# Branch B of a streaming layer: a segment's cast, subtraction and transfer given out two segments later

## The chip, the cores and the metric

The kernel runs on one core of a Trainium2 chip. The metric is device microseconds of one launch, as the median of several runs; lower is better. A profiled execution, taken by the hardware profiler, shows which engine did what and when: TensorE (PE), VectorE (DVE), ScalarE (ACT), GpSimd (POOL), and SyncE (SP), which issues the DMAs here.

## The reference, cut to what matters

One layer with two token mixers side by side. Branch A is a differential attention with softmax, branch B a stick-breaking attention; a gated merge and an output projection follow. There are 2048 prompt rows and 128 sample rows (8 running streams of 16). The change touches branch B's prompt rows alone:

```python
def stick_breaking_attention(q, k, v, qpos, kpos):
    z = jnp.einsum('bqhd,bkhd->bhqk', q, k,
                   preferred_element_type=jnp.float32) * (HEAD_DIM_B ** -0.5)
    mask = kpos[None, :] < qpos[:, None]
    log_1m = jnp.where(mask, jax.nn.log_sigmoid(-z), 0.0)
    log_a = jax.nn.log_sigmoid(z) + lax.cumsum(log_1m, axis=3, reverse=True) - log_1m
    a = jnp.where(mask, jnp.exp(log_a), 0.0)
    o = jnp.einsum('bhqk,bkhd->bqhd', a, v, preferred_element_type=jnp.float32)
    return o.astype(v.dtype)
```

In other words: the weight of key k is sigmoid(z_k) times the product of sigmoid(-z) over all later keys that the mask admits. The kernel computes that running product with a scan from the last key to the first.

## The kernel before

**Units and tiles.** The work is eight units, u = 0 to 7, one for each pair of heads (two of branch B, c = 0 and 1) and branch: the even ones are branch A, the odd ones branch B. A unit goes through 17 tiles of 128 rows, the sample tile (t = NT = 16) first and then t = 0 to 15. For each tile it projects, stores gates, and computes scores; tile t of the prompt has t + 1 key blocks of 128. While one unit's scores run, the projections of the next are interleaved, so that PE has other work between score matmuls; unit 7 is the last and has less of it. The second part of the kernel (branch and output projections, sample rows) follows unit 7 from about 1751 us on.

**One segment.** A head's keys are cut into segments of up to SEG = 8 blocks (1024 keys). A tile from 8 to 15 has two per head: segment 0 with 1024 keys, and segment 1 with the last 128 to 1024. A head's scores come in chunks of 512 keys from the last to the first; each goes through this chain:

- PE: score matmuls (L701, L702) into one of three PSUM banks `ps_s`
- ACT: two sigmoids (L599 and L600, shown as L135, since `act` records them): sigmoid(z) into the buffer `sc_p`, sigmoid(-z) back into the bank
- DVE: the scan (L675) of the bank into the buffer `sc_n`; a copy of one column (L674) carries it from segment 1 to segment 0

Behind a head's last chunk `stick_weights` is called for segment 1 and then segment 0: POOL multiplies `sc_p` by the shifted `sc_n` (L681). Then comes `turn`, which makes the weights ready for PE: ACT casts them to 16 bits (L609), DVE subtracts the cast from the exact weights (L612) for a low half, and SP issues a transposing DMA of both halves into `wt` (L619). From there PE multiplies with the values (L762, L763), 27 units of `later_on` behind (PV_LAG).

**What sets the order.** `later_on(lag, fn)` puts a piece of work on a list that `give` works off as work is given out; `spent` counts the cost of what has been given. `turn` is given out 1.5 plus up to 1 behind `stick_weights`; in unit 7 and for sample tiles at once. A scheduler then moves instructions within the dependencies; instructions marked `kept` stay in program order on their engine. The cast is kept for u < 7, the subtraction is not kept. The buffers `sc_p` and `sc_n` have 6 each, `wt` 5.

L725 is a gate's multiplication, L743 scales an output tile, L324 scales the values, L246 to L249 belong to later scales: all short DVE instructions that stand between scans and subtractions.

Of the kernel before, what the change touches and what calls it, by code (L numbers as in the profile page):

```python
# [22 lines left out]
ALU = mybir.AluOpType  # L23
# [10 lines left out]
NT = SEQ // P  # L34
# [5 lines left out]
SEG = 8  # L40
PV_LAG = 27.0
TURN_LAG = 1.5
B_LAG = 1.5
EXP_LAG = 1.0
SUM_LAG = 2.0
PIECE, CHUNK, PV_A, PV_B = 0.44, 0.22, 0.17, 0.085
# [79 lines left out]
def layer_kernel(ctx: ExitStack, tc: tile.TileContext, a: dict):  # L126
    nc = tc.nc
    V, S, G, T = nc.vector, nc.scalar, nc.gpsimd, nc.tensor
# [12 lines left out]
    def kept(x):  # L141
        tc.keep_in_program_order(x)
        return x
# [172 lines left out]
    def split(hi, lo, src, s, on=None):  # L316

        if on is S:
            S.activation(out=hi, in_=src, func=AF.Identity, scale=s)
        elif on is G:  # L320
            G.tensor_scalar(out=hi, in0=src, scalar1=s, scalar2=0.0, op0=ALU.mult, op1=ALU.add)
        else:
            V.tensor_scalar(out=hi, in0=src, scalar1=s, scalar2=None, op0=ALU.mult)
        V.scalar_tensor_tensor(out=lo, in0=src, scalar=s, in1=hi, op0=ALU.mult, op1=ALU.subtract)  # L324
# [277 lines left out]
    def turn(job, seg, scale=None):  # L602

        nb = seg["hi"] - seg["lo"]
        nk = nb * P
        w16 = seg["n"].bitcast(F16)
        hi, lo, src = w16[:, 0:nk], w16[:, nk : 2 * nk], seg["p"][:, 0:nk]
        if scale is None:
            x = S.copy(out=hi, in_=src)  # L609
            if job["t"] < NT and job["U"]["u"] < 7:  # L610
                kept(x)
            V.tensor_tensor(out=lo, in0=src, in1=hi, op=ALU.subtract)  # L612
        else:
            split(hi, lo, src, scale, S)
        if job["t"] == NT:
            seg["wt"] = job["pool"].tile([P, 10, P], F16, tag="dwt", name="dwt", bufs=2)
        else:
            seg["wt"] = wtp.tile([P, 2 * SEG, P], F16, tag="wt", name="wt", bufs=WT_BUFS)
        nc.sync.dma_start_transpose(out=seg["wt"][:, 0 : 2 * nb, :], in_=w16[:, 0 : 2 * nk])  # L619
        if job["t"] < NT:  # L620
            cost = (PV_A, PV_B)[job["U"]["kind"]]
            for fn in pv(job, seg):
                later_on(PV_LAG, fn, cost)

    def softmax_pair(job):
# [8 lines left out]
        def powers(i, c):  # L634
            seg = segs[i]
            w = seg[("p", "n")[c]][:, 0 : (seg["hi"] - seg["lo"]) * P]
            act(out=w, in_=w, func=AF.Exp, bias=nm[:, c : c + 1], accum_out=l[:, c, i : i + 1])
# [9 lines left out]
        def joined(seg):  # L647
            nk = (seg["hi"] - seg["lo"]) * P
            p, n = seg["p"][:, 0:nk], seg["n"][:, 0:nk]
            x = V.scalar_tensor_tensor(out=p, in0=n, scalar=r[:, 2:3], in1=p, op0=ALU.mult, op1=ALU.add)  # L650
            if job["t"] < NT:
                kept(x)

        stages = [(EXP_LAG, lambda i=i, c=c: powers(i, c)) for i in range(len(segs)) for c in range(2)]
        stages.append((EXP_LAG + SUM_LAG + 2.0 * n_all, sums))
        for i, seg in enumerate(segs):
            at = EXP_LAG + SUM_LAG + 2.0 * n_all + i
            stages += [(at, lambda seg=seg: joined(seg)), (at + TURN_LAG, lambda seg=seg: turn(job, seg, r[:, 0:1]))]
# [19 lines left out]
    def stick_weights(job, seg, later):  # L678
        m = (seg["hi"] - seg["lo"]) * P - (later is None)
        p, n = seg["p"], seg["n"]  # L680
        G.tensor_tensor(out=p[:, 0:m], in0=p[:, 0:m], in1=n[:, 1 : m + 1], op=ALU.mult)  # L681
        if job["t"] == NT or job["U"]["u"] == 7:
            turn(job, seg)
        else:
            later_on(B_LAG + m / 1024, lambda: turn(job, seg))

    def scores(U, t, jobs):

# [5 lines left out]
        def chunk(c, ch):  # L694
            job = own[c if kind == 1 else 0]
            seg = job["segs"][ch * 4 // SEG]
            n = 512 if ch < t // 4 else (t % 4 + 1) * P
            p = bank("s")
            qst, kk = U["q", t], U["k"][ch]
            diag = ch == t // 4  # L700
            T.matmul(p[:, 0:n], qst[:, c, :], kk[:, c, 0:n], start=True, stop=False)  # L701
            T.matmul(p[:, 0:n], qst[:, 2 + c, :], kk[:, c, 0:n], start=False, stop=not diag)  # L702
            if diag:
                m = mask_a if kind == 0 else mask_b
                T.matmul(p[:, n - m.shape[1] : n], idb, m, start=False, stop=True)  # L705
            evacuate(job, seg, c, p, ch * 512 - seg["lo"] * P, n, sc[:, 3:4], sc[:, 4:5], ch)
            if kind == 0:
                if diag and c == 1:
                    softmax_pair(job)
                return  # L710
            i = job["segs"].index(seg)
            later = job["segs"][i + 1] if i + 1 < len(job["segs"]) else None
            stick(seg, later, ch * 512 - seg["lo"] * P, n, p)
            if ch * 4 == seg["lo"]:
                if later is not None:
                    stick_weights(job, later, None)
                if i == 0:
                    stick_weights(job, seg, later)
# [48 lines left out]
    def later_on(lag, fn, cost=0.0):  # L767

        spent[1] += 1
        bisect.insort(due, (spent[0] + lag, spent[1], cost, fn))  # L770

    def pv(job, seg):

        U, t, c, i = job["U"], job["t"], job["c"], job["segs"].index(seg)
        last_seg = len(job["segs"]) - 1 if U["kind"] == 0 else 0
        first_seg = 0 if U["kind"] == 0 else len(job["segs"]) - 1
        nb = seg["hi"] - seg["lo"]

        def block(j):
            first, last = i == first_seg and j == 0, i == last_seg and j == nb - 1  # L780
            if first and (U["kind"] == 0 or c == 0):
                U["po", t] = bank("o")
            pv_block(job, seg, U["po", t], j, U["v"][seg["lo"] + j], first, last)
            if last and (U["kind"] == 0 or c == 1):
                store(U, t, natural(U, t, U.pop(("po", t))))

        return [lambda j=j: block(j) for j in range(nb)]
# [14 lines left out]
    def sample(U, dec, qpad, cs, vs, parity):  # L802
# [34 lines left out]
        def scores_all():  # L837

            box["jobs"] = [new_job(U, t, c, 5, dec) for c in range(heads)]
            qsam, kn = box["s"][:, 0:4, :], box["s"][:, 4:6, :]  # L840
            mask = mask_as if kind == 0 else mask_bs
            pn = bank("t")
            for c in range(2):
                p = pn[:, c * P : (c + 1) * P]
                T.matmul(p, qsam[:, c, :], kn[:, c, 0:P], start=True, stop=False)
                T.matmul(p, qsam[:, 2 + c, :], kn[:, c, 0:P], start=False, stop=False)
                T.matmul(p, idb, mask, start=False, stop=True)
            for c in range(2):
                pc = bank("s")
                for b in range(2):  # L850
                    for f in range(2):
                        for i in range(4):
                            T.matmul(pc[i * 32 : i * 32 + 32, :], qpad[:, f * 2 + c, 2 * i + b, :], box["k", i][:, b * 4 : b * 4 + 4, c, :],  # L853
                                     start=(b == 0 and f == 0), stop=(b == 1 and f == 1))
                job = box["jobs"][c % heads]
                seg = job["segs"][0]
                evacuate(job, seg, c, pn[:, c * P : (c + 1) * P], 512, P, sc[:, 3:4], sc[:, 4:5], 1)
                evacuate(job, seg, c, pc, 0, 512, box["f"][:, 0:1], box["f"][:, 1:2], 0)
                if kind == 1:
                    stick(seg, None, 512, P, pn[:, c * P : (c + 1) * P])  # L860
                    stick(seg, None, 0, 512, pc)
                    stick_weights(job, seg, None)
            if kind == 0:
                softmax_pair(box["jobs"][0])
# [550 lines left out]
    for n in range(len(steps) + 2):  # L1415
        made, qk, side = [], [], []
        if n < len(steps):
            u, t = steps[n]
# [16 lines left out]
        if at[0] == len(line) and not spare and not cached:  # L1435
            m = n - len(steps)
# [201 lines left out]
```

## Time and profile before

| | |
|---|---|
| median of 3 runs | 2212.37 us (2209.06 to 2217.97) |
| the profiled execution | 2207.3 us |
| its span, first to last instruction | 2205.4 us |
| mean granted TensorE clock | 0.984 |
| start of the first and the last subtraction of tiles 8 to 15 | 381.5 and 524.8 us (unit 1), 790.1 and 934.0 (3), 1197.3 and 1345.1 (5), 1606.8 and 1742.4 (7) |

The table of waits names first who waited, then, behind the arrow, what ended the wait. A row of the windows gives a stretch, its length and each engine's busy time in it. A row of the timeline gives start, duration, engine, line, operation, and in brackets how long its engine sat idle before it and what released it. Names have their buffer numbers left out.

### The profile page before, as it was taken

To read this page: it belongs to the slowest core of one execution; us is meant where nothing else is said; L and a number is where in the kernel's file an instruction comes from. 1 tells how busy PE (TensorE), PEld (TensorE's weight loads), DVE (VectorE), ACT (ScalarE), POOL (GpSimd) and SP (SyncE) were. 2 spreads that over 40 slices of the span, in tenths; PEclk is the share of its full clock that TensorE was granted. 3 is DMA by queue.
4 is the path that set the end of the run, shared out by engine and by line. 5 is a ranking of instruction groups with operands and counts; after the bars stand their busy time and mean duration, and the time that the engine had idled before them with its cause. 6 is when DMAs were issued, how large, how long until landed. Compare 5 with 4: busy or idle time off the path is not lost. (4 is left out here: it accounts for less than half of the span.)

```text
span 2205.4 us, 40973 instructions
## 1 busy us (share of the span) xinstructions
PE 2044.0 (93%) x14504; PEld 1091.4 (49%) x14504; DVE 1734.5 (79%) x3651; ACT 1598.9 (72%) x3080; POOL 726.7 (33%) x618
## 2 busy tenths in 40 slices
PE   3999999999999999999999998999997799999997
PEld 1545555555555455555555545455554344444443
DVE  5668868889877887987878887787789778778874
ACT  3977677788877777978687788875687656666641
POOL 0433024466301444742034464402344412112220
PEclk9999999999999999999999999999999899999999
DMA  9778668899797999978888899885777899998862
GB/s 331 259 249 191 132 151 231 184 222 206 199 243 174 221 191 208 214 197 216 204 223 202 186 229 217 216 198 123 171 154 157 204 254 222 245 246 236 227 161 67
DMA packets 820814, 449.96 MB, mean 204 GB/s; under 512 B 551962, under 2 KB 759114, under 8 KB 820096
## 3 DMA queue, kind: packets, MB, share of 16 engines
q1 hardware_dynamic: 819660, 446.96, 82.1%
q8 instruction: 113, 1.85, 0.3%
q14 instruction: 93, 0.76, 0.1%
q10 hardware_dynamic: 948, 0.39, 0.1%
HBM read 229.87 MB, written 86.02 MB: 143 GB/s over the span
## 5 line engine op out<-in xcount | busy, mean ns | idle before, releaser
L681 POOL TENSOR_TENSOR sc_p<-sc_p,sc_n 128x127 f32<-128x127 f32 (+7 forms) x192 | 319.3, 1665 | 557.8 <-DVE sc_n L675 528.4
L466 PEld LDWEIGHTS <-hs 128*128 128x128 f16 x3120 | 292.8, 99 | 316.8 <-issue 9.1
L466 PE MATMUL ps_mm<-wa,hs 128*128 128x512 f16 x1590 | 390.5, 381 | 6.8 <-DMA hs<-hT_d 3.7
L466 PE MATMUL ps_mm<-wb,hs 128*128 128x512 f16 x1530 | 380.9, 380 | 0.0
L675 DVE TENSOR_TENSOR_SCAN sc_n<-ps_s,sc_n,zero_t 128x512 f32<-128x512 f32 x192 | 245.3, 1278 | 40.3 <-ACT ps_s L135 34.5
L612 DVE TENSOR_TENSOR sc_n<-sc_p,sc_n 128x128 f16<-128x128 f32 (+7 forms) x192 | 224.7, 1173 | 39.3 <-ACT sc_n L609 38.5
L701 PE MATMUL ps_s<-k,qst 128*128 128x512 f16 (+3 forms) x640 | 223.1, 349 | 32.2 <-DVE sc_n L675 27.8
L540 PEld LDWEIGHTS <-hs 128*128 128x128 f16 x1632 | 155.3, 98 | 184.2 <-DVE qst L569 4.8
L540 PE MATMUL ps_t<-wa,hs 128*128 128x512 f16 x1020 | 243.4, 381 | 1.1 <-DVE qst L569 0.7
L135 ACT ACTIVATE sc_p<-ps_s,usc 128x512 f32<-128x512 f32 (+3 forms) x320 | 205.7, 643 | 45.6 <-PE ps_s L702 34.2
L702 PE MATMUL ps_s<-k,qst 128*128 128x512 f16 (+3 forms) x640 | 223.1, 350 | 0.0
L609 ACT CAST sc_n<-sc_p 128x128 f16<-128x128 f32 (+7 forms) x192 | 155.9, 814 | 87.4 <-POOL sc_p L681 86.8
L135 ACT ACTIVATE ps_s<-ps_s,usc 128x512 f32<-128x512 f32 (+3 forms) x320 | 198.0, 619 | 0.0
L540 PE MATMUL ps_t<-wb,hs 128*128 128x512 f16 x612 | 150.5, 382 | 6.2 <-DMA hs<-hT_d 2.6
L1533 PE MATMUL ps_o<-wo,wb 128*128 128x512 f16 x672 | 151.1, 380 | 0.7 <-ACT wb L1307 0.7
L762 PE MATMUL ps_o<-v,wt 128*128 128x128 f16 x1088 | 133.1, 223 | 19.6 <-DMA wt<-sc_n 18.9
L1538 POOL TENSOR_TENSOR x<-m,x 128x512 f32<-128x512 f32 x32 | 45.9, 1434 | 249.5 <-DVE m L1536 174.1
L595 DVE TENSOR_SCALAR_CACHE_REDUCE sc_p<-ps_s,usc 128x512 f32<-128x512 f32 (+3 forms) x160 | 106.2, 664 | 24.1 <-PE ps_s L702 18.2
L763 PE MATMUL ps_o<-v,wt 128*128 128x64 f16 x1088 | 124.2, 195 | 0.0
L595 DVE TENSOR_SCALAR_CACHE_REDUCE sc_n<-ps_s,usc 128x512 f32<-128x512 f32 (+3 forms) x160 | 106.3, 664 | 22.7 <-PE ps_s L705 11.7
L762 PEld LDWEIGHTS <-wt 128*128 128x128 f16 x1088 | 100.1, 100 | 48.3 <-DMA wt<-sc_n 24.1
L1499 PEld LDWEIGHTS <-wa 128*128 128x128 f16 x816 | 77.9, 99 | 92.6 <-issue 7.8
(373 smaller groups left out, 4451.0 us busy)
## 6 DMA issues: line engine op xcount, KB each, us to landing
hs<-hT_d SPq DMA_DIRECT2D x132, 512.0 KB, 4.7
g_d<-gt SPq DMA_DIRECT2D x68, 256.0 KB, 4.0
out_dram<-pr SPq DMA_DIRECT2D x204, 64.0 KB, 3.9
o_d<-o SPq DMA_DIRECT2D x136, 64.0 KB, 3.2
wa<-g_d SPq DMA_DIRECT2D x17, 512.0 KB, 6.8
wb<-g_d SPq DMA_DIRECT2D x17, 512.0 KB, 5.3
hs<-o_d SPq DMA_DIRECT2D x17, 512.0 KB, 3.8
wide<-in_w_ada_dram SPq DMA_DIRECT2D x8, 1024.0 KB, 11.8
```

What stands on the lines that cost most here:

```text
L135: i = S.activation(**kw)
L466: T.matmul(box["p"], box["h"][:, hi, k, :], U["w"][k][:, wi, :], start=(n == 0), stop=(n == 3 * KT - 1))
L540: x = T.matmul(box["g"][:, 0:gw], box["h"][:, hi, k, :], U["wg"][k // per][:, k % per, wi, :], start=(j == 0), stop=(j == 3 * KT - 1))
L595: V.tensor_scalar(out=dst[:, lo : lo + n], in0=p[:, 0:n], scalar1=sc_pos, scalar2=None, op0=ALU.mult, op1=ALU.max, accum_out=job["mx"][:, ...
L609: x = S.copy(out=hi, in_=src)
L612: V.tensor_tensor(out=lo, in0=src, in1=hi, op=ALU.subtract)
L675: V.tensor_tensor_scan(out=dst[:, lo : lo + n][:, ::-1], data0=src[:, 0:n][:, ::-1], data1=zero_t[:, 0:1].to_broadcast([P, n]), initial=fi ...
L681: G.tensor_tensor(out=p[:, 0:m], in0=p[:, 0:m], in1=n[:, 1 : m + 1], op=ALU.mult)
L701: T.matmul(p[:, 0:n], qst[:, c, :], kk[:, c, 0:n], start=True, stop=False)
L702: T.matmul(p[:, 0:n], qst[:, 2 + c, :], kk[:, c, 0:n], start=False, stop=not diag)
L762: T.matmul(po[:, c * P : (c + 1) * P], wt[:, wj, :], vt[:, c, :, :], start=first, stop=False)
L1533: T.matmul(po, st["y"][:, yi * 8 + k, :], wo[j * 4 + k // 2][:, wi, k % 2, :], start=(n == 0), stop=(n == 3 * KT - 1))
```

## The change

For tiles 8 to 15 of branch B, `turn` no longer goes to the list `due` (or, in unit 7, out at once). A list `held` takes the segments; whenever it has more than TURN_BEHIND = 2, the oldest is turned. A head's two segments are thus turned when the next head's are multiplied. Behind the unit's last segment the remaining two are given out as before. The cast is now kept in program order in unit 7 too, and the subtraction is kept, both for t >= 8. Tiles below 8 and the sample tile go as before.

```diff
+TURN_BEHIND = 2
...
             x = S.copy(out=hi, in_=src)
-            if job["t"] < NT and job["U"]["u"] < 7:
+            y = V.tensor_tensor(out=lo, in0=src, in1=hi, op=ALU.subtract)
+            if job["t"] < NT and (job["U"]["u"] < 7 or job["t"] >= SEG):
                 kept(x)
-            V.tensor_tensor(out=lo, in0=src, in1=hi, op=ALU.subtract)
+            if SEG <= job["t"] < NT:
+                kept(y)
...
         G.tensor_tensor(out=p[:, 0:m], in0=p[:, 0:m], in1=n[:, 1 : m + 1], op=ALU.mult)
-        if job["t"] == NT or job["U"]["u"] == 7:
+        if job["t"] == NT:
+            turn(job, seg)
+        elif job["t"] < SEG:
+            give_turn(job, seg)
+        else:
+            held.append((job, seg))
+            if len(held) > TURN_BEHIND:
+                turn(*held.pop(0))
+            if job["t"] == NT - 1 and job["c"] == 1 and seg["lo"] == 0:
+                while held:
+                    give_turn(*held.pop(0))
+
+    held = []
+
+    def give_turn(job, seg):
+
+        if job["U"]["u"] == 7:
             turn(job, seg)
         else:
-            later_on(B_LAG + m / 1024, lambda: turn(job, seg))
+            later_on(B_LAG + (seg["hi"] - seg["lo"]) / SEG, lambda: turn(job, seg))
```

What moves, first on DVE, in unit 3 around the first head of tile 13. Line numbers of the kernel before: L675 is the scan (a `128x256` one opens a head of this tile), L612 the subtraction, L568 and L569 copies of the next tile's keys and queries.

```order
L675 SCALAR_TENSOR_TENSOR sc_n<-ps_s,sc_n,zero_t 128x512
L674 COPY sc_n<-sc_n 128x1
L612 TENSOR_TENSOR sc_n<-sc_p,sc_n 128x1024
L568 COPY k<-ps_t 128x2x128
L569 COPY qst<-ps_t 128x512
L675 SCALAR_TENSOR_TENSOR sc_n<-ps_s,sc_n,zero_t 128x512 x2
L743 SCALAR_TENSOR_TENSOR o<-ps_o,usc_8072,ob 128x128
L612 TENSOR_TENSOR sc_n<-sc_p,sc_n 128x768
L675 SCALAR_TENSOR_TENSOR sc_n<-ps_s,zero_t 128x256
L324 SCALAR_TENSOR_TENSOR v<-ps_mm,usc_11034,v 128x2x64
L612 TENSOR_TENSOR sc_n<-sc_p,sc_n 128x1024
```

The same place in the changed kernel (the scan is L678 here, the subtraction L611, the copies L569 and L570):

```order
L678 SCALAR_TENSOR_TENSOR sc_n<-ps_s,sc_n,zero_t 128x512
L569 COPY k<-ps_t 128x2x128
L677 COPY sc_n<-sc_n 128x1
L570 COPY qst<-ps_t 128x512
L678 SCALAR_TENSOR_TENSOR sc_n<-ps_s,sc_n,zero_t 128x512 x2
L611 TENSOR_TENSOR sc_n<-sc_p,sc_n 128x640
L611 TENSOR_TENSOR sc_n<-sc_p,sc_n 128x1024
L678 SCALAR_TENSOR_TENSOR sc_n<-ps_s,zero_t 128x256
```

Before, single subtractions stand between scans, those of 768 and 1024 columns for the head that has just been scanned. Now a pair stands behind the head's last scan, and it is tile 12's second head's (640 and 1024 columns); the pair of the head just scanned follows one head later.

At the end of unit 7, on DVE, from the last head's second chunk on (L244 to L249 are short instructions for later scales):

```order
L675 SCALAR_TENSOR_TENSOR sc_n<-ps_s,sc_n,zero_t 128x512
L743 SCALAR_TENSOR_TENSOR o<-ps_o,usc_18672,ob 128x128
L674 COPY sc_n<-sc_n 128x1
L675 SCALAR_TENSOR_TENSOR sc_n<-ps_s,sc_n,zero_t 128x512
L612 TENSOR_TENSOR sc_n<-sc_p,sc_n 128x1024
L675 SCALAR_TENSOR_TENSOR sc_n<-ps_s,sc_n,zero_t 128x512
L612 TENSOR_TENSOR sc_n<-sc_p,sc_n 128x1024
L244 TENSOR_SCALAR sc_q<-ps_t 128x8
L246 TENSOR_SCALAR sc_f<-sc_q 128x8
L248 TENSOR_SCALAR sc_e<-sc_f 128x8
L249 TENSOR_SCALAR sc_e<-sc_f 128x8
L612 TENSOR_TENSOR sc_n<-sc_p,sc_n 128x1024
```

And in the changed kernel:

```order
L678 SCALAR_TENSOR_TENSOR sc_n<-ps_s,sc_n,zero_t 128x512
L677 COPY sc_n<-sc_n 128x1
L678 SCALAR_TENSOR_TENSOR sc_n<-ps_s,sc_n,zero_t 128x512
L245 TENSOR_SCALAR sc_q<-ps_t 128x8
L678 SCALAR_TENSOR_TENSOR sc_n<-ps_s,sc_n,zero_t 128x512
L247 TENSOR_SCALAR sc_f<-sc_q 128x8
L249 TENSOR_SCALAR sc_e<-sc_f 128x8
L611 TENSOR_TENSOR sc_n<-sc_p,sc_n 128x1024
L250 TENSOR_SCALAR sc_e<-sc_f 128x8
L611 TENSOR_TENSOR sc_n<-sc_p,sc_n 128x1024 x2
L762 SCALAR_TENSOR_TENSOR o<-ps_o,usc_18672,ob 128x128
L611 TENSOR_TENSOR sc_n<-sc_p,sc_n 128x1024
```

Four subtractions stand behind the last scan where two stood. SP's transfers for them move with them. Before, among its last issues (L1323, L548, L1317: loads and stores of other stages, L752: an output tile's store):

```order
L619 DMA_TRANSPOSE wt<-sc_n 128x16x128
L1323 DMA wb_1406<-g_d_97 128x2x512
L619 DMA_TRANSPOSE wt<-sc_n 128x16x128 x2
L548 DMA g_d_108<-gt_1396 128x512
L1317 DMA hs_181<-z_d_80 128x512
L752 DMA o_d_76<-o 128x128
L619 DMA_TRANSPOSE wt<-sc_n 128x16x128
```

And in the changed kernel, where the transfer is L622:

```order
L622 DMA_TRANSPOSE wt<-sc_n 128x16x128
L1342 DMA wb_1406<-g_d_97 128x2x512
L549 DMA g_d_108<-gt_1396 128x512
L622 DMA_TRANSPOSE wt<-sc_n 128x16x128 x4
L1336 DMA hs_181<-z_d_80 128x512
```

The last tile's four transfers now stand in a row, and one load and one store that stood ahead of the last of them come behind.

## The prediction

> **What bounds the kernel now.** I read the page's engine shares first, then the windows of the late tiles, where segments are longest, then what PE waited for in each of them.
>
> ```profile
> span 2205.4 us, 40973 instructions
> PE 2044.0 (93%) x14504; PEld 1091.4 (49%) x14504; DVE 1734.5 (79%) x3651; ACT 1598.9 (72%) x3080; POOL 726.7 (33%) x618
> ```
>
> PE is busy 2044.0 of 2205.4 us: 161 us are all that a change of order can win anywhere. The change touches only branch B's tiles 8 to 15, so the windows show how much of that lies there: tiles 8 to 11 of unit 1, tiles 12 to 15 of units 1 and 5, then unit 7 from tile 11 to its end, in two pieces (each row: window, its length, busy times, clock, DMA share, GB/s).
>
> ```profile
> core 0: us, PE busy (x) PEld busy (x) DVE busy (x) ACT busy (x) POOL busy (x), PEclk, DMA share, GB/s
> 373.80:439.80 66.00, 66.00 (x468) 35.05 (x467) 53.99 (x79) 50.08 (x96) 27.34 (x21) 1.00 0.83 193
> 439.80:518.90 79.10, 75.54 (x574) 41.30 (x572) 70.90 (x83) 71.22 (x132) 51.11 (x35) 1.00 0.96 214
> ...
> 1254.80:1335.50 80.70, 75.49 (x567) 40.74 (x564) 69.57 (x83) 71.31 (x132) 50.25 (x35) 1.00 1.00 210
> 1644.40:1716.10 71.70, 54.29 (x450) 30.53 (x447) 69.19 (x78) 55.54 (x101) 38.16 (x21) 0.95 0.73 155
> 1716.10:1751.00 34.90, 23.11 (x175) 13.05 (x176) 24.89 (x39) 20.88 (x31) 16.23 (x8) 0.80 0.84 179
> ```
>
> Tiles 8 to 11 have PE busy 66.00 of 66.00 us: nothing to win. In tiles 12 to 15, PE is idle for 3.6 us (unit 1) and 5.2 us (unit 5). In unit 7, with less other work for PE in between, DVE is busy 69.19 of 71.70 us (96%) and PE only 54.29. So units 1, 3 and 5 are bound by PE with small holes, unit 7 by DVE. What fills the holes, as waits of PE (us in all, times, longest), in the same order with unit 3 after unit 1, each over the tiles of its window and on to the unit's last PV matmuls:
>
> ```profile
> engine line waited for: us in total, times, longest us
> PE ps_s L701 <- DVE sc_n L675: 3.6, 5, 1.5
> PE ps_o L762 <- DMA wt<-sc_n: 2.3, 2, 1.3
> ...
> PE ps_s L701 <- DVE sc_n L675: 3.5, 4, 1.5
> PE ps_o L762 <- DMA wt<-sc_n: 0.3, 1, 0.3
> ...
> PE ps_o L762 <- DMA wt<-sc_n: 4.6, 5, 3.2
> PE ps_s L701 <- DVE sc_n L675: 3.9, 3, 1.5
> ...
> PE ps_s L701 <- DVE sc_n L675: 14.8, 17, 2.4
> PE ps_o L762 <- DMA wt<-sc_n: 11.7, 7, 2.9
> ```
>
> Two waits matter: a score matmul (L701) for a PSUM bank that a late scan (L675) still holds, and a PV matmul (L762) for a transfer (L619).
>
> **The change, part by part.** No instruction is added or removed; casts, subtractions and transfers move. Five terms.
>
> *1. Score stalls in units 1, 3 and 5.* Over the whole run ACT waits for POOL's product and DVE for ACT's cast:
>
> ```profile
> ACT sc_n L609 <- POOL sc_p L681: 86.8, 62, 6.9
> ...
> DVE sc_n L612 <- ACT sc_n L609: 38.5, 46, 2.0
> ```
>
> Such a wait holds up the scans queued behind it, as in unit 1, tile 13: the subtraction waits 1.83 us for its cast, and the next scan's bank comes 1.47 us late for PE.
>
> ```profile
> 474.73 1.75 DVE L612 TENSOR_TENSOR sc_n<-sc_p,sc_n 128x1024 f16<-128x1024 f32 x1 [1.83 <-ACT sc_n L609]
> ...
> 477.73 0.32 PE L701 MATMUL ps_s<-k,qst 128*128 128x384 f16 x1 [1.47 <-DVE sc_n L675]
> ```
>
> Given out one head later, product and cast are long done when the subtraction's turn comes, so the stalls of 3.6 + 3.5 + 3.9 = 11.0 us lose their cause. What is late next is the first scan of the next head, since both subtractions now stand ahead of it. PE's scores run three banks ahead (the three `ps_s` banks), so the fourth score of the next head meets the pause. From a head's last score it takes two sigmoids, the last scan, the pause (4.3 us, term 2) and the next scan:
>
> ```profile
> L675 DVE TENSOR_TENSOR_SCAN sc_n<-ps_s,sc_n,zero_t 128x512 f32<-128x512 f32 x192 | 245.3, 1278 | 40.3 <-ACT ps_s L135 34.5
> ...
> L135 ACT ACTIVATE sc_p<-ps_s,usc 128x512 f32<-128x512 f32 (+3 forms) x320 | 205.7, 643 | 45.6 <-PE ps_s L702 34.2
> ```
>
> Twice 0.64 for the sigmoids, 1.28, 4.3 and 1.28 make 8.1 us. A head has four chunks here, so its fourth score comes about one head's time after the last one: 79.10 us for eight heads, 9.9 us each. The pause fits on average, with 1.8 us to spare; in the shorter heads it won't. I let 4 of the 11 us come back: **term 1 is -7**, between -11 (all gone) and 0 (the pause stalls as often as the casts did).
>
> *2. DVE against POOL in units 1, 3 and 5.* These rows show the price of a subtraction beside a POOL product. In unit 7, a subtraction that starts just ahead of a product runs 1.22 us and the product takes 3.03; another that starts behind a product takes 2.60. In unit 1, the short L725, 0.27 us where it is free (the first row), takes 2.09 behind subtraction and product. A product alone takes 2.00.
>
> ```profile
> 1680.62 0.27 DVE L725 TENSOR_TENSOR gt<-gt,r 128x128 f32<-128x128 f32 x1
> 1680.80 1.22 DVE L612 TENSOR_TENSOR sc_n<-sc_p,sc_n 128x1024 f16<-128x1024 f32 x1
> ...
> 1685.86 2.60 DVE L612 TENSOR_TENSOR sc_n<-sc_p,sc_n 128x1024 f16<-128x1024 f32 x1
> 1680.85 3.03 POOL L681 TENSOR_TENSOR sc_p<-sc_p,sc_n 128x1024 f32<-128x1024 f32 x1 [3.04 <-DVE sc_n L675]
> ...
> 440.34 2.09 DVE L725 TENSOR_TENSOR gt<-gt,r 128x128 f32<-128x128 f32 x1
> ...
> 451.40 2.00 POOL L681 TENSOR_TENSOR sc_p<-sc_p,sc_n 128x1024 f32<-128x1024 f32 x1 [2.43 <-DVE sc_n L675]
> ```
>
> So the two don't run side by side, and the first subtraction wins. Behind every late head the program now has: last scan, first subtraction (free), second subtraction, while the last scan has released POOL's product. The second one waits for the product's end: 1.38 us over its own 1.22 by the 2.60 row, 1.8 by the 3.03 row (0.05 + 3.03 - 1.22 = 1.86). I take 1.7, so the pause is 1.22 + 1.7 + 1.22 = 4.1 to 4.3 us, and eight heads lose 13.6 us. What the subtractions lose now is in their own windows (DVE time of L612, then of L725):
>
> ```profile
> 439.80:518.90 79.10, 23.97 (x16) 1.00 0.96 214
> ...
> 1254.80:1335.50 80.70, 22.59 (x16) 1.00 1.00 210
> 1644.40:1716.10 71.70, 27.86 (x16) 0.95 0.73 155
> 1716.10:1751.00 34.90, 8.06 (x6) 0.80 0.84 179
> ...
> 439.80:518.90 79.10, 2.88 (x4) 1.00 0.96 214
> ```
>
> Unit 1's 16 are nine of 1024 columns (9 x 1.22) and seven with 5120 columns together (at 1.22 / 1024 each, 6.1): 17.1 free, so 6.9 us are lost now; unit 5 loses 5.5. L725 loses 2.88 less four times about 0.27, 1.8 us, and mostly would not any more, as it now stands behind both subtractions. DVE's work thus grows by 13.6 - 6.9 - 1.8 = 4.9 us in unit 1 (unit 3 alike) and 6.3 in unit 5, 16.1 in all. DVE has 8.2 us free in unit 1 and 11.1 in unit 5, which hides most; it would be (70.90 + 4.9) / 79.10 = 96% busy. I let a quarter through: **term 2 is +4**, between 0 and 16.
>
> The Trainium skill, "SBUF — State Buffer", section "Who interferes with whom", speaks against the change more strongly: the port pair that DVE and GpSimd share is an exclusive lock, held for the whole instruction by whoever issued first. By that rule the product would begin only after the first subtraction and cost the second the full 2.00 us; the trace agrees nearly, since 0.05 + 3.03 falls 0.14 us short of 1.22 + 2.00. At 0.3 us more per head, over eleven heads of unit 7 in full and a quarter of 24 others, the sum would be about +9.
>
> *3. Transfers at a unit's end.* All of a head's transfers are issued a head later, so behind the unit's last scan four stand in a row on SP. One takes about 2.5 us of queue (two took 5.06):
>
> ```profile
> 1737.19 5.06 SPq L619 DMA_TRANSPOSE wt<-sc_n  x2
> 1744.41 3.24 SPq L619 DMA_TRANSPOSE wt<-sc_n  x1
> ...
> 1737.09 1.27 DVE L675 TENSOR_TENSOR_SCAN sc_n<-ps_s,sc_n,zero_t 128x512 f32<-128x512 f32 x1
> ...
> 1739.79 2.46 DVE L246 TENSOR_SCALAR sc_f<-sc_q 128x8 int32<-128x8 int32 x1
> ...
> 1742.44 1.23 DVE L612 TENSOR_TENSOR sc_n<-sc_p,sc_n 128x1024 f16<-128x1024 f32 x1
> ...
> 1749.54 0.29 PE L762 MATMUL ps_o<-v,wt 128*128 128x128 f16 x1 [2.88 <-DMA wt<-sc_n]
> ```
>
> Four take 10 us, at a DMA share that is already 0.96 to 1.00. Unit 5 has five such waits now, 4.6 us, 0.9 each. The PV lag of 27 covers the rest; I add one such wait per unit: **term 3 is +3**, between 0 and 4.6 per unit.
>
> In the Trainium skill, "DMA: Bandwidth & Descriptors", section "🔬 Latency and other measured facts", transposing transfers reach 261 GB/s, and more where contiguous. By that there is room above the 210 GB/s of unit 5, and the term is 0; the trace's share of 1.00 at 210 says there is none. The sum would be +1.
>
> *4. Unit 7's stretch.* No cast wait to speak of is to be won here, as it turned at once. Its 16 subtractions should take 15.9 us (eight wide ones, 9.8, and 5120 columns, 6.1) and take 27.86: 12.0 lost now; the last six lose 0.8 (8.06 against 7.3). Eleven late heads at 1.7 make 18.7, so DVE gains 5.9 us of work, less some 2.3 for the tiny L246 (2.46 us in the rows of term 3), which the last product holds up now. With DVE at 96% all of it is on the path: **term 4 is +3.6**, between 0 and 6.
>
> *5. Unit 7's end.* Now the last scan ends at 1738.36 and the last subtraction at 1743.67, the transfer is issued at 1744.41, and PV starts at 1749.54, 5.1 us later (rows of term 3). In the changed order the last scan has two subtractions fewer ahead of it (2.4 us earlier, at 1.22 each), but four subtractions and four transfers behind it: the last transfer begins some 8.8 us after that scan (1.3 + three times 2.5) where it was 6.0. That cancels: **term 5 is 0**, between -1 and +4.
>
> Sum: -7 + 4 + 3 + 3.6 + 0 = about **+4 us** on the profiled execution's 2207.3 (span 2205.4), 2211.3. The median of the three runs is 5.1 higher than that execution, so 2216.4 as a median: **2216**. About 0.5% (11 us) is what a measurement of this kernel can tell from no change.
>
> **The rivals.**
>
> *N, hidden anyway.* PE is full, holes close and open elsewhere: within 3 us of 2207.3, 2212 as a median. For it: 66.00 of 66.00. Against it: unit 7, where DVE bounds.
>
> *S, DVE becomes the bound (slower).* The second subtraction waits for the product behind every late head, and DVE in units 1, 3 and 5 turns into what unit 7 shows, where at 96% busy PE waits 14.8 us for scans. It decides from the point where scans, subtractions and 1.7 us of waiting exceed a head's 9.9 us. Then term 1 is 0 and the DVE growth is all on the path: 16.1 + 3.6 + 3 = +22.7, 2230, as a median 2235. Against it: by the sum DVE still has 4% left.
>
> *T, transfers pile up.* 4.6 us in each of four units in place of term 3: -7 + 4 + 18.4 + 3.6 = +19, 2226, median 2231. For it: the share of 1.00. Against it: unit 3's 0.3 us at nearly the same load.
>
> *F, faster.* POOL starts its product only behind both subtractions (its release takes longer than 1.22 us), so nothing is lost to it: unit 7 gets most of its 12.0 us back, say 10, and term 1 stays: -17, 2190, median 2195. Against it: in the 1680.85 row the product started 0.05 us behind the subtraction.
>
> **How the numbers follow.** Forecast 0.44 (its own range, by terms 1 and 2, 2205 to 2226), N 0.22, S 0.16, F 0.12, T 0.06. Faster by over 0.5%: most of F, 0.10. Slower: S, T and the top of the forecast, 0.24. Within: 0.66. The range reaches from 2202 (half of F's gain) to 2238 (above S); F's lower half and an S with late transfers on top, under 2 in 10, are left out.
>
> **What would show it.** In the changed profile: L609's wait for L681 and L612's for L609 nearly gone (term 1); L612's 1024 columns in two kinds behind each scan, 1.2 and about 2.9 us, 30 us of L612 per 16 in place of 24 (term 2); L701's waits in units 1, 3 and 5 at 4 us in place of 11 (term 1); L762's 1 us more per unit (term 3); DVE above 97% in unit 7 (term 4). A pair of subtractions at 1.2 each, or L701's waits over 15 us, would make it wrong.

## The result, and the profile after

| | before | changed |
|---|---|---|
| median | 2214.11 us (6 runs, 2209.06 to 2217.97) | 2233.11 us (6 runs, 2228.36 to 2241.11) |
| ratio | | 1.0091, 95% interval 1.0072 to 1.0110 |
| profiled execution (span) | 2207.3 us (2205.4) | 2241.1 us (2239.0) |

The change makes the kernel 0.9% slower, some 19 us. The profiled execution of the changed kernel is the slowest of its six, 8 us above the median, and that of the kernel before lies 7 us below its median; so the two traces differ by 34 us where the medians differ by 19. Small differences between them carry no weight. Nor is all of the 34 us waiting: by the page below PE is busy 17.5 us longer with the same 14504 matmuls (2061.5 against 2044.0), at a mean granted clock of 0.975 against 0.984, and idle 16 us longer (177.5 against 161.4). In the medians the clock hardly differs: its mean is 0.979 over the changed kernel's six executions and 0.981 over 29 of the kernel before.

The page of the changed kernel first: the span, the engines, and the groups of the subtraction (L611 now) and the cast (L610), which answer to L612 and L609 of before.

```profile
span 2239.0 us, 40964 instructions
PE 2061.5 (92%) x14504; PEld 1099.5 (49%) x14504; DVE 1767.7 (79%) x3651; ACT 1596.9 (71%) x3080; POOL 716.8 (32%) x618
...
L611 DVE TENSOR_TENSOR sc_n<-sc_p,sc_n 128x128 f16<-128x128 f32 (+7 forms) x192 | 259.1, 1372 | 15.2 <-ACT sc_n L610 15.1
...
L610 ACT CAST sc_n<-sc_p 128x128 f16<-128x128 f32 (+7 forms) x192 | 148.4, 813 | 43.7 <-POOL sc_p L684 43.6
```

What the change was to do, it did: ACT waits 43.6 us for the product instead of 86.8, and DVE 15.1 us for the cast instead of 38.5. And the price shows as well: the same 192 subtractions take 259.1 us instead of 224.7. The windows hold the same pieces of work as in the prediction, from and up to where PE has streamed as many columns: tiles 12 to 15 of units 1 and 5 and unit 7's late tiles, then the time of L611 in units 1, 3, 5 and 7 (each row as in the prediction):

```profile
440.80:520.80 80.00, 75.55 (x571) 40.93 (x570) 73.45 (x84) 69.14 (x132) 50.11 (x37) 1.00 0.99 215
...
1261.60:1346.30 84.70, 78.77 (x571) 42.90 (x570) 71.74 (x84) 68.97 (x132) 50.89 (x36) 0.96 1.01 212
1664.30:1740.20 75.90, 58.54 (x443) 32.39 (x442) 73.44 (x78) 56.36 (x103) 36.79 (x23) 0.89 0.68 146
...
440.80:520.80 80.00, 28.74 (x16) 1.00 0.99 215
850.90:931.30 80.40, 28.74 (x16) 1.00 1.01 218
1261.60:1346.30 84.70, 27.65 (x16) 0.96 1.01 212
1664.30:1740.20 75.90, 30.62 (x18) 0.89 0.68 146
```

28.7 us for 16 subtractions where 24.0 stood, with DVE busy 73.45 of 80.00 us (92%, and 90% before). The timeline of one late head of unit 1 shows why: two subtractions behind the last scan, 640 and 1024 columns, together 3.74 us where they would take 2.0, beside a product that is released with them.

```profile
462.32 3.74 DVE L611 TENSOR_TENSOR sc_n<-sc_p,sc_n 128x640 f16<-128x640 f32 x2
...
462.55 2.43 POOL L684 TENSOR_TENSOR sc_p<-sc_p,sc_n 128x1024 f32<-128x1024 f32 x1 [3.24 <-DVE sc_n L678]
```

PE's waits in units 1, 3, 5 and 7, each from the start of its window to the unit's last PV matmuls:

```profile
PE ps_s L720 <- DVE sc_n L678: 3.0, 4, 1.6
PE ps_t L541 <- DVE qst L570: 1.1, 1, 1.1
PE ps_o L781 <- DMA wt<-sc_n: 0.6, 1, 0.6
...
PE ps_s L720 <- DVE sc_n L678: 2.7, 3, 1.6
PE ps_o L781 <- DMA wt<-sc_n: 1.2, 1, 1.2
...
PE ps_s L720 <- DVE sc_n L678: 4.8, 5, 1.7
PE ps_o L781 <- DMA wt<-sc_n: 0.6, 1, 0.6
...
PE ps_s L720 <- DVE sc_n L678: 15.4, 13, 3.0
PE ps_o L781 <- DMA wt<-sc_n: 13.2, 5, 9.1
```

In units 1, 3 and 5 PE waits for scans as long as before (10.5 us against 11.0) and less for transfers (2.4 against 7.2). A new wait is that for the copies of the next tile's queries (L570), 1.1 us in each of the three, where the kernel before shows none in these windows. In unit 7 the waits are a little longer (15.4 against 14.8 and 13.2 against 11.7), with one of 9.1 us at the end:

```profile
1759.45 3.05 DVE L611 TENSOR_TENSOR sc_n<-sc_p,sc_n 128x1024 f16<-128x1024 f32 x1
...
1759.42 2.00 POOL L684 TENSOR_TENSOR sc_p<-sc_p,sc_n 128x1024 f32<-128x1024 f32 x1 [2.30 <-DVE sc_f L247]
...
1762.53 9.64 SPq L622 DMA_TRANSPOSE wt<-sc_n  x4
...
1766.97 0.29 PE L781 MATMUL ps_o<-v,wt 128*128 128x128 f16 x1 [9.09 <-DMA wt<-sc_n]
```

That wait ends 4.4 us after the first of the four transfers is issued, so it is not the four in a row that PE waits for here, but the first of the four subtractions, which stands behind the last scan and takes 3.05 us beside a product, and its transfer. The other three add short waits behind it.

These waits alone don't account for 19 us. So I compared where time goes by work: PE does the same 14504 matmuls in both, and for each stretch of the kernel before I took the time that another kernel needs until its PE has streamed as many columns. The table gives the excess in us, worked out from the matmuls' starts in the traces. "Own" stretches hold tiles 8 to 15 of units 1, 3, 5 and 7; in the others nothing is held. The runs of the experiments stand in it too.

| stretch of before, us | 374-545 own (1) | 545-777 | 777-955 own (3) | 955-1186 | 1186-1365 own (5) | 1365-1600 | 1600-1755 own (7) | 1755-2190 |
|---|---|---|---|---|---|---|---|---|
| changed | 2.6 | 1.2 | -0.1 | 2.4 | 5.6 | 5.3 | 5.6 | 10.3 |
| only unit 7 | 0.1 | -0.6 | -1.5 | 0.9 | -0.4 | 1.6 | 8.0 | 5.2 |
| all but unit 7 | 4.0 | 0.4 | 0.3 | -0.2 | 3.5 | 1.1 | -1.2 | 4.6 |
| tile 15 plain | 2.6 | 7.6 | -0.2 | 5.4 | 6.8 | -0.7 | 10.7 | -1.7 |
| one per segment | 7.0 | 9.0 | 5.3 | 14.3 | 5.8 | -2.0 | 0.2 | 4.1 |
| unit 7, one per segment | 1.2 | -0.8 | 0.4 | -0.2 | -1.8 | 0.4 | -1.2 | 6.3 |
| unit 7, tile 15 plain | -1.1 | 2.1 | 3.7 | 0.6 | -0.4 | -0.3 | 7.5 | 1.3 |
| before, lag 2.0 | 5.7 | 2.7 | 4.9 | 5.6 | 6.9 | 8.6 | 5.0 | 4.4 |
| unit 7, one per segment, behind 1 | 1.8 | -0.1 | 0.8 | 1.9 | -0.6 | 2.8 | -6.6 | 2.6 |
| before, A's lag 1.25 | 1.7 | 3.0 | 0.1 | 3.9 | -2.3 | 0.6 | -3.3 | 4.3 |
| all, one per segment, behind 1 | 1.1 | 10.7 | 1.2 | 10.5 | -1.9 | 3.4 | -7.1 | 5.9 |
| before, lag 1.0 | 5.0 | -1.1 | 3.4 | -0.1 | 5.1 | -5.4 | -1.7 | -0.5 |
| before, kept order alone | 2.5 | -0.1 | -0.2 | 0.6 | 0.3 | -1.0 | -3.3 | 6.7 |

The kernels that touch unit 7 alone, and the one with the kept order alone, have, by their traces, PE's matmuls in the same order as the kernel before up to 1600 us. Their first six columns (-1.8 to 3.7) are therefore what one execution differs from another by. In the last column nearly all stand above zero, as the profiled execution of before lies below its median; its PE is also the least busy of all the traces (2044.0 us, the others 2048.9 to 2063.4).

### The profile page after: what moved, and what is told of

It is laid out like the page before. It is cut to its first block, busy times and chain, and to the rows that moved or that the text cites. A ratio compares the mean times of both kernels' runs of the same rounds, so it can differ in the third digit from the quotient of the medians.

```text
span 2239.0 us, 40964 instructions
## 1 busy us (share of the span) xinstructions
PE 2061.5 (92%) x14504; PEld 1099.5 (49%) x14504; DVE 1767.7 (79%) x3651; ACT 1596.9 (71%) x3080; POOL 716.8 (32%) x618
## 5 line engine op out<-in xcount | busy, mean ns | idle before, releaser
L467 PEld LDWEIGHTS <-hs 128*128 128x128 f16 x3120 | 292.6, 99 | 323.4 <-issue 15.1
L678 DVE TENSOR_TENSOR_SCAN sc_n<-ps_s,sc_n,zero_t 128x512 f32<-128x512 f32 x192 | 245.7, 1279 | 51.0 <-ACT ps_s L136 42.3
L611 DVE TENSOR_TENSOR sc_n<-sc_p,sc_n 128x128 f16<-128x128 f32 (+7 forms) x192 | 259.1, 1372 | 15.2 <-ACT sc_n L610 15.1
L610 ACT CAST sc_n<-sc_p 128x128 f16<-128x128 f32 (+7 forms) x192 | 148.4, 813 | 43.7 <-POOL sc_p L684 43.6
```

Source lines behind the costliest of these rows:

```text
L467: T.matmul(box["p"], box["h"][:, hi, k, :], U["w"][k][:, wi, :], start=(n == 0), stop=(n == 3 * KT - 1))
L611: y = V.tensor_tensor(out=lo, in0=src, in1=hi, op=ALU.subtract)
L678: V.tensor_tensor_scan(out=dst[:, lo : lo + n][:, ::-1], data0=src[:, 0:n][:, ::-1], data1=zero_t[:, 0:1].to_broadcast([P, n]), initial=fi ...
```

## The experiments

**Which units.** The first two kernels split the change by unit.

```diff
-        elif job["t"] < SEG:
+        elif job["t"] < SEG or job["U"]["u"] < 7:
             give_turn(job, seg)
```

(the second has `== 7` there; in each the order of casts and subtractions is kept as in the changed kernel where it holds, and as before elsewhere).

> Units 1, 3 and 5 give out their segments as before the change; only unit 7 holds them. The change as a whole costs about 19 us. Theory LOCK (the second subtraction of each pair waits for POOL's product, and DVE, full in these stretches, passes it on; all units alike): unit 7 has 16 of 64 late heads but the fullest DVE, so +5 to +8 us over the kernel before. Theory END (what costs is the four segments that pile up behind a unit's last scan): unit 7's end shows one PV wait of 9 us, so +8 to +11. Theory CLOCK (PE's lower granted clock behind longer idle stretches, mostly after unit 7): +12 or more.

> Units 1, 3 and 5 hold their segments as in the changed kernel; unit 7 gives them out at once as before. LOCK: +11 to +14 us over the kernel before. END: +8 to +11 (three unit ends of about 3 to 4 each). CLOCK: +7 or less. If the shares of this run and of the one with unit 7 alone add up to about 19, the units don't depend on each other.

Measured: unit 7 alone 1.0045 (1.0025 to 1.0065), 10 us; the other three 1.0049 (1.0027 to 1.0071), 10 us. They add up to the change. Unit 7, with a quarter of the heads, costs half. Both figures fit the theory of the end (8 to 11 each) and lie just outside that of the pairs (5 to 8, and 11 to 14). The theory of the clock (12 or more, and 7 or less) fits neither, and the mean granted clock over the executions is 0.981 in both kernels and in the kernel before.

Where the second kernel loses its 10 us is less clear. In the table 4.0 and 3.5 of them stand in the own stretches of units 1 and 5 and next to nothing in branch A's; but in its trace PE is idle only 2.2 us longer than before (163.6 against 161.4 us), and busy 11.9 us longer, at a clock of 0.979.

**The end or the pairs.** The next two take away one suspect each over all units. In the first, tile 15 turns as before (its casts and subtractions are ordered as before, too), so no pile is left at a unit's end:

```diff
-        elif job["t"] < SEG:
+        elif job["t"] < SEG or job["t"] == NT - 1:
+            while held:
+                turn(*held.pop(0))
             give_turn(job, seg)
...
-            if job["t"] == NT - 1 and job["c"] == 1 and seg["lo"] == 0:
-                while held:
-                    give_turn(*held.pop(0))
```

> As the changed kernel, but tile 15 turns as before, so nothing is left over behind a unit's last scan; tiles 8 to 14 keep the held pairs. END: at least 12 of the 19 us come back, +7 or less over the kernel before; the PV wait of 9 us at unit 7's end is gone. LOCK: only the pairs of tile 15 are gone (8 of 64 heads) and 14 us or more of the 19 stay.

In the second, segment 1's product is given out behind its own last scan, so that one subtraction stands behind each segment, meant to come ahead of the product that is released there:

```diff
             if ch * 4 == seg["lo"]:
-                if later is not None:
-                    stick_weights(job, later, None)
-                if i == 0:
-                    stick_weights(job, seg, later)
+                stick_weights(job, seg, later)
```

> As the changed kernel, with one edit: POOL's product of segment 1 is given out behind that segment's own last scan instead of behind the head's, so that of the two held segments one is turned behind each segment's last scan. No pair stands in a row, each subtraction comes ahead of the product that its scan releases, and the delay of two segments and the left-over pile at a unit's end stay. LOCK: L612's time in the late windows falls from 28.7 to about 20 us per 16, and 10 us or more of the 19 come back. END: the time stays within 4 us of the changed kernel's.

Measured: 2243.33 us, ratio 1.0145 (1.0117 to 1.0174), and 2249.72 us, 1.0173 (1.0136 to 1.0209). The first refutes the theory of the end, the second that of the pairs, and neither theory foresaw that both kernels would be slower than the changed one. Yet the second kernel did with the subtractions what was expected, as its window of unit 1 shows (L611, then PE's only wait there, and then ACT's longest in the branch A stretch that follows):

```profile
439.20:517.70 78.50, 19.25 (x16) 1.00 0.96 210
...
PE ps_s L720 <- DVE sc_n L678: 3.2, 4, 1.7
...
ACT junk L300 <- DMA wb<-in_w_in_dram: 10.7, 1, 10.7
```

19.25 us for 16 subtractions instead of 28.74, the window a little shorter (78.5 us; 80.0 in the changed kernel, 79.1 before), and PE's waits for scans unchanged. So 9.5 us less of blocked subtractions go with a window only 1.5 us shorter in unit 1, where PE is the bound. Units 3 and 5 are no such clean test: there 17 subtractions still take 24.4 and 23.4 us, and the windows are 82.5 and 83.4 us long (80.4 and 84.7 in the changed kernel). The largest losses come behind the window in unit 1 and in branch A's stretches, 9.0 and 14.3 us, in which nothing was held; there ACT waits 10.7 us for a load of weights, though whether PE pays for that wait isn't shown. The pairs alone don't explain this, and a third theory was needed, that the change alters the order of what follows.

**Unit 7 by itself.** Here everything ahead of 1600 us stays the same, so the two first theories can be tested cleanly. The edits are those of the last two, with `job["U"]["u"] == 7` beside them.

> Only unit 7 holds its segments (the run with unit 7 alone cost +10 us), and there the product of segment 1 is given out behind its own last scan, so that one subtraction, not a pair, stands behind each segment's last scan. Nothing else in the program moves ahead of unit 7's tile 8. LOCK (second subtraction of a pair behind POOL's product): L612's time in unit 7's late tiles falls by about 10 us and the loss before the last tile, 5 to 6 us, is gone: +3 to +5 over the kernel before, what the four left-over segments at the end cost. END: as with unit 7 alone, +8 to +11.

> Only unit 7 holds its segments, in pairs, but tile 15 turns as before, so that only one head's two segments are left behind the last scan. LOCK: tiles 8 to 14 still lose 5 us, +5 to +8 over the kernel before. END: the PV wait of 9 us at the end is gone, +0 to +3. Together with the run of one subtraction per segment: if the two gains add up to 10, both causes share unit 7's loss.

Measured: 1.0022 (1.0007 to 1.0036) with one subtraction per segment, 1.0058 (1.0040 to 1.0076) with tile 15 plain. The first, 5 us, meets the theory of the pairs. The second, 13 us, refutes the theory of the end and lies above what the pairs alone were to leave (5 to 8): the one wait of 9 us is gone from its trace (the longest for a transfer is 3.8 us) and nothing is won. Unit 7's late tiles, the time of L611 in them, and PE's waits from there to the unit's end, for unit 7 alone with pairs and then with one subtraction per segment:

```profile
1647.30:1724.40 77.10, 57.62 (x443) 31.85 (x442) 74.65 (x78) 57.37 (x105) 37.39 (x23) 0.89 0.70 144
...
1647.30:1724.40 77.10, 31.90 (x18) 0.89 0.70 144
...
PE ps_s L720 <- DVE sc_n L678: 16.2, 11, 3.2
PE ps_o L781 <- DMA wt<-sc_n: 12.2, 4, 9.2
```

```profile
1645.90:1714.80 68.90, 54.01 (x444) 29.39 (x443) 65.92 (x78) 57.34 (x104) 42.05 (x23) 0.97 0.80 164
...
1645.90:1714.80 68.90, 19.91 (x17) 0.97 0.80 164
...
PE ps_o L783 <- DMA wt<-sc_n: 14.8, 8, 3.8
PE ps_s L720 <- DVE sc_n L678: 6.8, 9, 1.6
```

1.77 us per subtraction with pairs, 1.17 without; waits for scans 16.2 against 6.8, the same piece of work 77.1 against 68.9 us (before: 71.70, with 14.8 us of waits over both pieces). That is the mechanism: in unit 7, where DVE is full, the second subtraction's wait for the product is paid in full. The stretch is as long as DVE is busy plus 2.4 to 3.0 us in the kernel before (71.7 and 69.19), in the changed one (75.9 and 73.44) and in these two, while PE is busy only about three quarters of it. The granted clock doesn't set it: at 0.93 this piece of work took 77.4 us with tile 15 plain and 70.1 us in the last run below. What remains are 14.8 us of waits for transfers in the second run; that they come from the pile at the end is tried with the faster version below.

**The order of the rest.** The third theory needs kernels that hold nothing. First the kernel before with `B_LAG` at 2.0 and at 1.0 instead of 1.5.

> The kernel before with one number changed: the turn of branch B's segments is given out 2.0 instead of 1.5 units behind the product (units 1, 3 and 5; unit 7 as before). No pairs, no holding, no left-over pile. LOCK and END: within 3 us of the kernel before. Theory RESHUFFLE (in units 1, 3 and 5 the cost is not in what was moved but in the order of everything given out afterwards, which any shift changes, branch A's units included): 5 us or more away, more likely slower, and the loss lies in branch A's stretches too.

> The same with 1.0 instead of 1.5 units. LOCK and END: within 3 us of the kernel before. RESHUFFLE: 5 us or more away, with the loss spread over stretches in which no turn was moved.

Measured: 2254.1 us, ratio 1.0209 (1.0180 to 1.0237) at 2.0, and 1.0028 (1.0016 to 1.0041) at 1.0. Half a unit later costs 43 us, more than the change, without a pair or a pile. Some of it goes with a lower clock, 0.972 in all four executions against 0.981 before; how much, isn't shown. Some of it may be the later turn itself, in units 1, 3 and 5; but there is loss where none is given out by that lag. Unit 7's tiles 6 to 11, which turn at once in both, and in which PE had no idle time in the kernel before (first row), take 71.80 us in the kernel with 2.0 (second), and PE waits there for loads of activations:

```profile
1580.00:1645.00 65.00, 65.00 (x455) 34.51 (x453) 53.01 (x78) 51.91 (x105) 23.10 (x20) 1.00 0.75 161
```

```profile
1615.40:1687.20 71.80, 66.45 (x458) 34.72 (x457) 55.25 (x76) 50.97 (x101) 28.63 (x21) 1.00 0.65 146
...
PE ps_mm L466 <- DMA hs<-hT_d: 3.1, 3, 1.6
```

The kernel with 1.0 speaks less for the third theory: it is slower by some 6 us, as that theory had it, but by the table its loss lies in the own stretches of units 1, 3 and 5 (5.0, 3.4 and 5.1), where the turn was moved, and not in branch A's.

Two controls: the kept order of casts and subtractions alone (the third part of the change, nothing held), and a quarter of a unit on `TURN_LAG`, branch A's own lag, with branch B's code untouched.

> The kernel before with the third part of the change alone: casts (unit 7 too) and subtractions of branch B's tiles from 8 on stay in program order; nothing is held, every turn is given out when it was. LOCK and END: within 3 us of the kernel before. RESHUFFLE: 5 us or more away if the scheduler had moved many of these subtractions; if not, the order hardly changes and neither does the time.

> The kernel before with one number of branch A changed: TURN_LAG 1.25 instead of 1.5, a quarter of a unit earlier for the casts and subtractions of branch A's weights. Nothing of branch B is touched directly. LOCK and END say nothing of it: within 3 us. RESHUFFLE: 5 us or more away from the kernel before, on either side, with shifts in branch B's stretches as well.

Measured: 0.9997 (0.9985 to 1.0010) for the kept order, so that part costs nothing, and by the traces it leaves PE's order alone up to 1600 us; and 1.0025 (1.0012 to 1.0038) for the quarter unit, 5.5 us slower. A shift of a lag is worth this much without anything held. None of these shifts is neutral, though: `turn` also gives out the PV matmuls, so a later turn moves them on PE too.

**A version that is faster.** In unit 7 alone, one subtraction per segment, and `TURN_BEHIND = 1`, so that less is left at the end:

> Only unit 7 holds, one subtraction behind each segment's last scan as in the run before, but held back by one segment instead of two, so that at the end of the unit two subtractions instead of three or four are left behind the last scan. LOCK: L612's mean stays near 1.2 us in unit 7's late tiles and PE's waits for scans stay near 8 us. END: what is left of that run's loss (about 4 us) goes with the pile; the time is within 3 us of the kernel before, or below it by up to 3. If it stays 4 us or more above, the rest of the loss is not at the end of unit 7 but in what follows it.

Measured: 2209.48 us against 2212.37 (12 and 29 runs), ratio 0.9980 (0.9967 to 0.9992): 3 us faster than the kernel before by the medians, 4 by the ratio, and some 24 faster than the changed kernel. The same rows as above:

```profile
1651.90:1722.30 70.40, 26.33 (x16) 0.95 0.76 162
...
PE ps_s L720 <- DVE sc_n L678: 12.0, 8, 2.9
PE ps_o L783 <- DMA wt<-sc_n: 4.3, 6, 1.8
```

The expectation of the subtractions missed: at 1.65 us each they are nearly as slow as before (1.74), since now one often starts behind a product. The gain shows at the end, 4.3 us of waits for transfers where there were 11.7 before and 14.8 with two segments held, and in somewhat fewer waits for scans. It is small: the kernel with the kept order alone had a median of 2210.93 us. Then the same for all four units:

> All four units of branch B as unit 7 in the run that was faster than the kernel before: one subtraction behind each segment's last scan, held back by one segment, tiles 8 to 15. LOCK: no subtraction waits for a product any more, so units 1, 3 and 5 gain as unit 7 did: 4 to 10 us below the kernel before. RESHUFFLE: L612's time in units 1, 3 and 5 falls just as far (to about 18 us per 16), PE's waits for scans there fall too, but the loads, stores and transfers behind them come in another order and the time is 5 us or more above the kernel before.

Measured: 2232.87 us, ratio 1.0100 (1.0065 to 1.0134). Unit 7 gains as before (-7.1 us in the table), units 1, 3 and 5 stay about where they were in their own stretches (1.1, 1.2, -1.9), and 10.7 and 10.5 us are lost between them. L611 fell to 21.8 us in unit 1 but not in unit 5 (27.1), so the run was not as clean a test of the pairs as meant. But it shows most plainly that time can be lost in stretches in which nothing is held.

## Why the prediction was right or wrong

The median of 2233 us lies inside the range given, near its top, but not in the forecast's own range (2205 to 2226): the sum gave +4 us and some 19 came. A slowdown clear of noise had 0.24, most of it for the rivals S and T. That the number lies in the range is thus partly luck, for the sum that led to it had three of five terms wrong and left one thing out. Of the signs that were named, one came plainly: the subtractions' 30 us per 16. The score waits of 4 us didn't come (10.5), nor did DVE above 97% in unit 7 (73.44 of 75.90 us, 96.8%).

**Term 1, stalls in units 1, 3 and 5 (-7): wrong.** The waits for casts did go, yet 10.5 of 11.0 us of score stalls are still there. The pause was sized rightly (3.74 us for 640 and 1024 columns, about 4.1 to 4.3 for two wide ones). The step that failed is "The pause fits on average, with 1.8 us to spare": one stall was replaced by another. By the traces, DVE stood idle for 9.5 us ahead of unit 1's 32 subtractions of tiles 8 to 15 before, and these took 42.4 us; now it is idle for 0.0, and they take 52.4. In unit 3 it was 6.0 and 42.5 us and is 0.0 and 52.5, in unit 5 5.1 and 41.0 against 0.0 and 51.2. What the waits for casts gave back, the waits for products took, and more. In which heads the pause doesn't fit stays open.

**Term 2, DVE against POOL (+4): right in mechanism and in DVE's size, wrong in price.** L612 was to take 30 us per 16; it took 28.7, 28.7 and 27.7. But the run with one subtraction per segment took 9.5 us out of unit 1's, and PE's waits for scans stayed the same. So little of it reaches PE in unit 1, whose window became 1.5 us shorter; for units 3 and 5 that isn't shown.

**Term 3, transfers at a unit's end (+3): wrong in sign.** PV waits in units 1, 3 and 5 went from 7.2 to 2.4 us.

**Term 4, unit 7's stretch (+3.6): right, and a little small.** The traces give 5.6 us in the changed kernel and 8.0 in unit 7 alone, its end included, and taking away the pairs took the loss away: the 32 subtractions of tiles 8 to 15 took 44.4 us before, 52.9 with pairs and 39.6 with one per segment. **Term 5, its end (0):** the transfers' waits grew from 11.7 to 13.2 us, as one long wait instead of several. Near enough; what the term did not have is that holding one segment instead of two gains there.

**What the sum left out.** It began with "casts, subtractions and transfers move", and priced everything else at nothing. But `turn` also gives out the PV matmuls, PV_LAG behind itself, so they move as well: in the later half of each of units 1, 3 and 5 they stand about 10,000 columns of other matmuls further back in PE's order, some 4 us of PE's work. And `give` places all that follows by what it was given before. In the traces PE's own order differs in every 50 us from 400 to 1850 us, in branch A's units as well.

Of the changed kernel's 19 us about 10 are unit 7's. About half of these go with the pairs (10 us with them, 5 without), by the mechanism of term 4. The other half goes, and some more, when one segment is held instead of two; taking tile 15's pile away with the pairs left gained nothing, so the pile's own share is open. The other 10 us belong to units 1, 3 and 5, and their cause stays open. The pairs cost PE little in unit 1; kernels without any held segment became 5 to 43 us slower by a shifted lag, and kernels with other edits to the turn lost up to 14 us in single stretches in which nothing was held, which speaks for the order of the rest. But the run that holds in these units alone shows its excess in their own stretches, so later PV matmuls or DVE's late copies may be a direct price. No run holds the segments and keeps the rest of the order. Nor is it settled which instructions' new places cost what: loads of weights and activations on SP's queue, for which ACT and PE waited in the slowest runs, are among those that the traces name.

**Rival S** had the mechanism of unit 7, but put 16.1 of its 22.7 us into the wrong units: DVE, busy 92% of unit 1's window and 85% of unit 5's, didn't become the bound there. That its 2235 lies 2 us from the median is luck. **Rival F** fails by the 3.05 and 3.74 us rows: the pair is not free there. **Rivals N and T** fail too: the time moved, and the waits for transfers in units 1, 3 and 5 fell.

## What to carry to other kernels

A wait that disappears pays only on the engine that sets the end; look at what the moved work now stands beside. One subtraction to each product instead of two gained in unit 7, where DVE was the bound; given to all units the same edit lost 1.0 to 1.7% against the kernel before. Where a scheduler orders everything, a small edit to one stage changes the order of all that follows, and such a kernel should be tried with other small shifts before a difference of 1% is put down to the edit's purpose. List also what the moved piece of code gives out behind itself, here the PV matmuls. Confine the edit to the last stage, behind which little is left to be disturbed, if that is where the bound is.

## What the runs showed of the hardware

DVE's subtraction and POOL's product kept each other out in both directions within one program. A subtraction of 640 columns, 0.23 us ahead of a product, ran first (0.80 us), and the one of 1024 behind it took 3.02 us while the product ran; a subtraction 0.03 us behind a product (1759.45 against 1759.42) took 3.05 us beside the product's undisturbed 2.00. The Trainium skill, "SBUF — State Buffer", section "Who interferes with whom", says that issue order, not the kind of operation, decides who blocks, and these rows agree. What was not expected is how little it takes: by the recorded starts a few hundredths of a microsecond decide whether DVE pays 1.8 us or POOL 1.0 (the 3.03 us row of the prediction). A scan, whose data come from PSUM, took 1.28 us beside a product (1755.28), no more than its mean over the run. Four transposing transfers in a row occupied SP's queue for 9.64 us, 2.4 each, and the load behind them was issued at 1772.22 us, right after the last.
